# A hybrid decoder layer on one core: the mixers' small matmuls gathered in fewer places between the projections

## The chip, the cores and the metric

One core of a Trainium2 chip runs the whole layer as one program. The metric is device time in microseconds (us): the median of several executions of the program. The kernel before takes 152.27 us (three executions, 151.97 to 152.85).

## What is computed

One post-norm decoder layer on 256 tokens of width 1024, in float32. A first layer norm gives h; one input projection (1024 to 3844 columns) feeds four causal mixers of four heads each: a Mamba-2 SSD, HGRN2, RetNet retention and MoBA attention. Their outputs, each gated with SiLU, are put side by side and go through one output projection, and the result is normed with the residual.

```python
h = _layernorm(x, emb_ln_g, emb_ln_b)
proj = einsum('bld,dn->bln', h, w_in)
(s_z, s_xbc, s_dt, h_q, h_f, h_i, h_g, r_q, r_k, r_v, r_g,
 m_q, m_k, m_v, m_g) = split(proj)
y_cat = concatenate([_ssd(...), _hgrn2(...), _retention(...), _moba(...)])
out = _layernorm(ALPHA * h + einsum('blm,md->bld', y_cat, w_out), ln_g, ln_b)
```

## The kernel before

TensorE (PE in the profile) does two kinds of work. The projections are exact float32 products put together from three float32r products each (high part of x with high part of w, low with high, high with low): per half unit of 128 output columns or tokens, 8 k tiles times 3 matmuls of 128 x 256, recorded at line 406 as `pj_<unit>`. The mixers' own matmuls are small and in plain float32: attention scores, products with the values, transposes. Most use a half-width or half-height tile of the array (128 x 64, 64 x 64 or 64 x 128 in the profile's column behind the names); the transposes (`mpt`, `xst`, `yt`) and the segment sums (`seg`, `ecum`) use the whole 128 x 128.

The order of the work is written by hand and kept as written. The program walks through slots 0 to 29, one per half unit of the input projection, and then through the output projection, with a slot ahead of every second piece of it. `begin(slot)` first sends the load of a weight half six half units ahead (`load_w`, line 205, on SyncE's queue SP, five buffers), then splits the weight half four ahead into its high part (`split_hi`, line 222, on ScalarE, ACT) and, after the mixers' steps, its low part (`split_lo`, line 231, on VectorE, DVE). Between the two it runs the steps that the table `steps` lists for this slot. Then `project(slot)` emits the 24 matmuls. Each engine takes its instructions in this order, and waits on semaphores for what it reads and for the release of buffers. PSUM has eight banks, handed out in turn to whatever asks next; a bank is reused once its last reader is done.

The names that matter below, with their lines: `hgrn_diag` (486, output `pc`), `moba_tr(j)` (848: four transposes of the probabilities `pe` into a PSUM bank, `mpt`) and `moba_tr_in(j)` (852: ACT copies that bank out), `ssd_xt` (748, `xst`), `ssd_seg` (714 and 717, `seg`, `ecum`, which read `ra` from GpSimd, POOL, line 693), `ssd_scores_in` (734 `sm` on DVE, 736 `scx` on ACT), `hgrn_av` (438, `hgo`), `moba_av` (869, `mbo`), `ssd_av` (762 `ssy`, 766 `sso`), `ret_q` (895, `rq`), `ret_scores_in` (922, `rat`), `y_transpose` (417, `yt`) and `ret_av` (438, `reo`). The retention's decay table is loaded by `ret_load` (line 892) on the SP queue; its tile shares its memory with `pe`:

```python
    pe = sb([P, 3 * NH, P], "pe", tag="xt0")
...
    ret = sb([P, 2, 2, SEQ], "ret", tag="xt0")
...
    def ret_q():
        nc.vector.tensor_mul(rq, ps_of["r_q"], ret[:, 0])
```

Of the kernel before, what the change touches and what calls it, by code (L numbers as in the profile page):

```python
# [29 lines left out]
# Order of the branches in the output projection.  # L30
ORDER = [0, 1, 3, 2]

# Columns of w_in by unit, in the order of their use.
# [27 lines left out]
# Rows that are the same for every token.  # L61
# [10 lines left out]
# Column pieces of the output projection by token tile: the last ones are the smaller.  # L72
OCOLS = [(0, 512, 1024), (0, 512, 768, 1024)]

# Per-channel parameters: emb_g, emb_b (k tiles), conv_w (4 taps, 4 tiles), conv_b, lb logits.
# [3 lines left out]
# Shape constants.  # L79
# [40 lines left out]
def hybrid_layer(  # L120
# [49 lines left out]
    # The tensor engine runs at half its clock until it has been busy for some microseconds:  # L170
    # products of a cleared tile keep it so while x comes in.
# [11 lines left out]
    # The weights stream in halves of a unit; each half is split exactly into two float32r  # L183
    # parts. Those of the output projection also take the place of spent mixer tiles.
# [147 lines left out]
    ps_of, hq = {}, {}  # L332

    def first_unit():
        """Both halves of unit 0 side by side, as the k tiles come in."""
        ps = [bank(f"pj_h_f{n}")[:, :SEQ] for n in range(2)]
        ps_of["h_f", 0], ps_of["h_f", 1] = ps

        def part(k, q):
            l = (whi, whi, wlo)[q][0, k // 4][:, k % 4]  # L340
            r = (hhi, hlo, hhi)[q]
            for n in range(2):
                nc.tensor.matmul(ps[n], l[:, n * P:(n + 1) * P], r[:, k, :], start=(k == 0 and q == 0),  # L343
                                 stop=(k == KT - 1 and q == 2))
        for k in range(KT):
            if k < 4:
                h_transpose(k + 4, 0)
                h_transpose(k + 4, 1)
                h_in(k + 4)
            if k == 1:  # L350
                split_hi(0, 1, 2, (1,), nc.vector.tensor_copy)
            part(k, 0)
            if k:
                part(k - 1, 1)
        part(KT - 1, 1)
        split_lo(0, 0, 2, (1,))
        split_lo(0, 1, 2)
        split_hi(1, 0)
        split_hi(1, 1)
        project(2, (0, 1))  # L360
        for k in range(KT):
            part(k, 2)
        project(3, (0, 1))

    def project(slot, parts=(0, 1, 2)):
        """Half a unit: 128 columns (channels on partitions) or 128 tokens."""
# [45 lines left out]
    def y_transpose(y, idx):  # L412
        """y [tokens, T, 256] -> the two k tiles of y_cat, channels on partitions."""
        b = bank(f"yt{idx}").rearrange("p (a t) -> p a t", a=2)
        for j in range(2):
            for T in range(NT):
                nc.tensor.transpose(b[:, j, T * P:(T + 1) * P], y[:, T, j * P:(j + 1) * P], ident)
        ytb[idx] = b
# [6 lines left out]
    def hs(t, h, lo_, n_):  # L425
        """head h of [128 channels on two tiles, tokens]"""
        r = 64 * (h % 2)
        return t[r:r + 64, h // 2, lo_:lo_ + n_]
# [21 lines left out]
    # Softmax over the single layer, cumulated, less its first row.  # L450
# [23 lines left out]
    # The attention within 64 tokens is built level by level: at level m the keys of an  # L474
    # even block of m tokens meet the queries of the odd block that follows. Heads by
    # parity: index (h % 2, T, h // 2); each parity has its own PSUM bank.
# [149 lines left out]
    def conv(n, name):  # L626
        """causal convolution of channel tile n, straight from the projection"""
        ps = ps_of[name][:, n % 2, :]
        if n % 2 == 0:
            acc[name] = sb([P, 2, SEQ], f"cacc_{name}", tag="cacc", bufs=2)  # L630
        a_ = acc[name][:, n % 2, :]

        def tap(i):
            return ch[:, C_CW + 4 * i + n:C_CW + 4 * i + n + 1]
        nc.scalar.activation(a_, ps, AF.Identity, scale=tap(3), bias=ch[:, C_CB + n:C_CB + n + 1])  # L635
        for d in range(1, 4):
            nc.vector.scalar_tensor_tensor(a_[:, d:], ps[:, :SEQ - d], tap(3 - d), a_[:, d:],  # L637
                                           op0=ALU.mult, op1=ALU.add)
# [20 lines left out]
    def ssd_step_a():  # L659
        # softplus(u) = max(u, 0) + log1p(e), e = exp(-|u|); log1p(e) = 2 atanh(e / (2 + e))  # L660
        au = sb([P, 8], "au")
        sd["ex"] = sb([P, 8], "ex")
        sd["ea"] = sb([P, 4], "ea")
        nc.vector.scalar_tensor_tensor(au, u, -1.0, u, op0=ALU.mult, op1=ALU.max)
        nc.scalar.activation(sd["ea"], row("alog"), AF.Exp)
        nc.scalar.activation(sd["ex"], au, AF.Exp, scale=-1.0)

    def ssd_step_b():
# [22 lines left out]
        # operands of the segment sums: sum over r of [r > s] [r <= l] a_r  # L691
# [169 lines left out]
    def moba_av():  # L861
        """channels on partitions: what the output projection takes"""
# [104 lines left out]
    po = {}  # L967

    def oproj(i, T, c0, c1):
        """branch i's share of 128 tokens by columns c0 .. c1 (within 512)"""  # L970
# [18 lines left out]
    def out_norm(T):  # L989
# [9 lines left out]
        for cs in cuts:  # L999
# [5 lines left out]
    # Steps taken in each slot before its half unit of projection: what a step reads was  # L1005
    # put in order at least a slot before, so that the tensor engine does not wait for it.
# [4 lines left out]
        6: [lambda: hgrn_diag(qk, 0), moba_load],  # L1011
        7: [lambda: hgrn_diag(e1, 8), lambda: level(2), h_values, hgrn_diag_in],
# [12 lines left out]
        17: [lambda: load_rows(0), ssd_step_a, ssd_step_b, lambda: moba_tr(0)],  # L1025
        18: [level128, moba_v, ssd_scores, lambda: moba_tr(1), lambda: moba_tr_in(0), level128_in, ssd_scores_in],
        19: [ssd_xt, lambda: moba_tr(2), lambda: moba_tr_in(1)],
        20: [ssd_seg, ssd_exp, lambda: moba_tr_in(2), lambda: hgrn_av(0), lambda: hgrn_av(1),
             ret_load],
        21: [ret_q, ssd_xt_in, ssd_mask, hgrn_norm, moba_av, lambda: residual(0)],  # L1030
        22: [ssd_av, ret_k, lambda: residual(1), lambda: load_rows(2)],
        23: [ssd_gate, ssd_norm],
        24: [ret_v, ret_scores, ret_cross, ssd_out, ret_scores_in, ret_cross_in],
        25: [lambda: y_transpose(sy.rearrange("p (t h) d -> p t (h d)", t=2), 0),
             lambda: ret_av(0), lambda: ret_av(1)],
        26: [lambda: y_split(0), hgrn_out],
# [82 lines left out]
```

## Time and profile before

| | |
|---|---|
| executions | 152.27, 152.85, 151.97 us; median 152.27 |
| profiled execution, first to last instruction (span) | 150.6 us |
| PE busy | 138.5 us (92%), 1320 matmuls |
| DVE busy | 116.5 us (77%), 240 instructions |
| ACT busy | 74.8 us (50%), 120 instructions |
| POOL busy | 17.8 us (12%), 23 instructions |
| DMA | 26.07 MB, mean 173 GB/s |

The page of the profile gives the profiled execution by its span, 150.6 us, and no other time for it; the median of the runs lies 1.65 us above that span. Busy times of engines overlap each other, so they don't add up to the span. Rows of the timeline give start, duration, engine, line, operation, output and inputs, the tile of the array that a matmul uses, the shape, and how many equal instructions the row stands for; a wait before it stands in brackets. The end of a matmul in the trace is modelled, so durations of neighbours overlap, and the start of the next one is the better measure of what one costs.

### The profile page before, as it was taken

The numbers are of one execution on the slowest core, as the hardware profiler recorded it, in microseconds if no ns is written. First come the engines' busy times: TensorE is split into PE (matmuls) and PEld (weight loads), VectorE is DVE, ScalarE is ACT, GpSimd is POOL, SyncE is SP. The second block draws the span as 40 slices with busy tenths as digits, with TensorE's granted clock in tenths as the row PEclk, the third lists the DMA queues.
The fourth block names the chain that finished last, engine by engine and source line by source line (L and its number), as shares of the span: only waits on it lengthen the run. The fifth ranks groups of instructions, "written<-read, shape, count | busy, mean of one in ns | idle before, by whom it ended". The sixth has DMA issues, their size and how long they took to land.

```text
span 150.6 us, 3259 instructions
## 1 busy us (share of the span) xinstructions
PE 138.5 (92%) x1320; PEld 127.7 (85%) x1320; DVE 116.5 (77%) x240; ACT 74.8 (50%) x120; POOL 17.8 (12%) x23
## 2 busy tenths in 40 slices
PE   6859999999999999999999999998999999999900
PEld 3149999999999998999999999997999988888800
DVE  2589968988596397969899999859379899168681
ACT  3079978552451759699919722062663764000000
POOL 4230000000000000000062063050004000004040
PEclk9986999999999999999999999999999999999995
DMA  4998299998748431656517800689804450000304
GB/s 151 275 406 324 69 325 325 307 327 319 197 133 255 138 80 59 168 189 232 190 65 256 308 0 0 159 310 364 270 23 139 140 139 4 0 0 0 139 0 139
DMA packets 9390, 26.07 MB, mean 173 GB/s; under 512 B 1056, under 2 KB 1696, under 8 KB 9120
## 3 DMA queue, kind: packets, MB, share of 16 engines
q1 hardware_dynamic: 9376, 25.87, 52.2%
q8 instruction: 10, 0.16, 0.4%
q14 instruction: 4, 0.03, 0.1%
HBM read 24.82 MB, written 1.05 MB: 172 GB/s over the span
## 4 chain that ended last, share of the span: by engine, by line
PE 56%; DVE 20%; ACT 8%; DMA 6%; issue 3%; POOL 2%; SPq 1%; POOLq 1%; DVEq 0%; ACTq 0%
PE po L979 5%; PE po L980 5%; PE po L978 5%; PE pj_h_f L343 4%; PE pj_m_q L406 4%; PE pj_xs L406 4%; PE pj_m_k L406 4%; PE pj_m_g L406 4%; PE pj_h_q L406 4%; PE pj_h_i L406 4%; PE pj_r_g L406 4%; DMA xt<-in_x_dram 3%; DMA ret<-in_ret_dram 3%; PE pj_bc L406 2%; ACT pe L842 2%
## 5 line engine op out<-in xcount | busy, mean ns | idle before, releaser
L979 PE MATMUL po<-wlo_wo,yhi 128*128 128x512 f32 (+1 forms) x40 | 14.0, 349 | 0.0
L978 PE MATMUL po<-whi_wo,yhi 128*128 128x512 f32 (+1 forms) x40 | 14.0, 349 | 0.0
L980 PE MATMUL po<-whi_wo,ylo 128*128 128x512 f32 (+1 forms) x40 | 13.9, 347 | 0.0
L222 ACT CAST whi_wo<-wr_wo 128x1024 fp32r<-128x1024 f32 x8 | 8.3, 1047 | 5.3 <-PE pj_h_g L406 2.2
L231 DVE TENSOR_TENSOR wlo_wo<-wr_wo,whi_wo 128x1024 fp32r<-128x1024 f32 x8 | 9.6, 1218 | 0.0
L693 POOL TENSOR_SCALAR_AFFINE_SELECT ra<-ahi 128x1024 fp32r<-128x1024 f32 x1 | 1.1, 1101 | 65.6 <-DVE ahi L689 65.6
L978 PEld LDWEIGHTS po<-whi_wo,yhi 128*128 128x128 f32 x40 | 7.5, 188 | 1.0
L980 PEld LDWEIGHTS po<-whi_wo,ylo 128*128 128x128 f32 x40 | 7.5, 188 | 1.0
L979 PEld LDWEIGHTS po<-wlo_wo,yhi 128*128 128x128 f32 x40 | 7.5, 188 | 1.0
L986 DVE TENSOR_TENSOR xn<-xn,po 128x512 f32<-128x512 f32 (+1 forms) x5 | 2.9, 579 | 5.8 <-PE po L980 5.8
L176 PE MATMUL warm<-warm 128*128 128x512 f32 x6 | 5.5, 1082 | 1.5 <-DVE warm L173 1.5
L637 DVE SCALAR_TENSOR_TENSOR cacc_xs<-pj_xs,ch,cacc_xs 128x255 f32<-128x255 f32 (+2 forms) x6 | 2.9, 482 | 4.6 <-ACT cacc_xs L635 4.4
L300 PEld LDWEIGHTS tr<-ck,xn 128*128 128x128 f32 x16 | 2.3, 171 | 4.1 <-DVE xn L276 4.1
L300 PE MATMUL tr<-ck,xn 128*128 128x128 f32 x16 | 3.6, 351 | 2.3 <-DVE xn L276 2.3
L263 DVE BATCH_NORM_STATS2 lst<-xt 128x6 f32<-128x512 f32 x4 | 2.8, 694 | 3.6 <-DMA xt<-in_x_dram 3.6
L842 ACT ACTIVATE pe<-pe,mmax 128x128 f32<-128x128 f32 (+1 forms) x8 | 3.5, 445 | 3.0 <-DVE mmax L835 3.0
L176 PEld LDWEIGHTS warm<-warm 128*128 128x128 f32 x6 | 1.8, 326 | 3.6 <-issue 2.1
L222 ACT CAST whi_h_f<-wr_h_f 128x512 fp32r<-128x512 f32 x3 | 1.9, 617 | 6.1 <-DMA wr_h_f<-in_w_dram 6.1
L406 PE MATMUL pj_h_g<-whi_h_g,hhi 128*128 128x256 f32 x16 | 4.7, 294 | 0.0
L406 PE MATMUL pj_m_q<-hhi,whi_m_q 128*128 128x256 f32 x16 | 4.7, 293 | 0.0
L406 PE MATMUL pj_r_k<-hhi,whi_r_k 128*128 128x256 f32 x16 | 4.7, 293 | 0.0
L406 PE MATMUL pj_m_v<-whi_m_v,hhi 128*128 128x256 f32 x16 | 4.7, 292 | 0.0
(298 smaller groups left out, 544.7 us busy)
## 6 DMA issues: line engine op xcount, KB each, us to landing
wr_wo<-in_wo_dram SPq DMA_DIRECT2D x8, 512.0 KB, 4.0
rb<-in_rows_dram SPq DMA_DIRECT2D x2, 1024.0 KB, 7.7
wr_z<-in_w_dram SPq DMA_DIRECT2D x2, 520.0 KB, 6.3
xt<-in_x_dram SPq DMA_DIRECT2D x4, 256.0 KB, 3.4
wr_h_f<-in_w_dram SPq DMA_DIRECT2D x4, 256.0 KB, 5.2
wr_h_q<-in_w_dram SPq DMA_DIRECT2D x2, 512.0 KB, 5.2
wr_h_i<-in_w_dram SPq DMA_DIRECT2D x2, 512.0 KB, 5.0
wr_m_q<-in_w_dram SPq DMA_DIRECT2D x2, 512.0 KB, 4.9
```

The costliest lines, as they stand in the source:

```text
L176: nc.tensor.matmul(wb, warm[:, :P], warm, start=True, stop=True)
L222: copy(whi[i, j][:, r, :], t[:, r, :])
L231: nc.vector.tensor_sub(wlo[i, j][:, r, :], t[:, r, :], whi[i, j][:, r, :].bitcast(F32))
L300: nc.tensor.transpose(trb[k][:, T * P:(T + 1) * P], xn[T][:, k * P:(k + 1) * P], ident)
L343: nc.tensor.matmul(ps[n], l[:, n * P:(n + 1) * P], r[:, k, :], start=(k == 0 and q == 0), stop=(k == KT - 1 and q == 2))
L406: nc.tensor.matmul(ps, l, r, start=(n == 0), stop=(n == len(seq) - 1))
L637: nc.vector.scalar_tensor_tensor(a_[:, d:], ps[:, :SEQ - d], tap(3 - d), a_[:, d:], op0=ALU.mult, op1=ALU.add)
L842: nc.scalar.activation(pt[:, h, :], pt[:, h, :], AF.Exp, bias=mmax[:, i:i + 1], accum_out=msum[:, i:i + 1])
L978: nc.tensor.matmul(po[T, c0], yhi[:, k, ts], hi, start=(i == 0 and j == 0), stop=False)
L979: nc.tensor.matmul(po[T, c0], yhi[:, k, ts], lo, start=False, stop=False)
L980: nc.tensor.matmul(po[T, c0], ylo[:, k, ts], hi, start=False, stop=(i == 3 and j == 1))
L986: nc.vector.tensor_add(xn[T][:, cs], xn[T][:, cs], po[T, cs.start])
```

## The change

Only the table `steps` is edited (and comments are dropped). The first `hgrn_diag` goes from slot 6 to 7; `moba_tr(0)` and its copy from 17 and 18 to 18; `moba_tr_in(1)` from 19 to 18; `ssd_xt` and `moba_tr(2)` from 19 to 20; `moba_av` from 21 to 22; `y_transpose` of the SSD output and `ret_av` from 25 to 26. No instruction is added or removed. Small matmuls stood ahead of sixteen half units of the input projection, and now stand ahead of twelve; the one place within the output projection stays.

```diff
-        6: [lambda: hgrn_diag(qk, 0), moba_load],
-        7: [lambda: hgrn_diag(e1, 8), lambda: level(2), h_values, hgrn_diag_in],
+        6: [moba_load],
+        7: [lambda: hgrn_diag(qk, 0), lambda: hgrn_diag(e1, 8), lambda: level(2), h_values,
+            hgrn_diag_in],
...
-        17: [lambda: load_rows(0), ssd_step_a, ssd_step_b, lambda: moba_tr(0)],
-        18: [level128, moba_v, ssd_scores, lambda: moba_tr(1), lambda: moba_tr_in(0), level128_in, ssd_scores_in],
-        19: [ssd_xt, lambda: moba_tr(2), lambda: moba_tr_in(1)],
-        20: [ssd_seg, ssd_exp, lambda: moba_tr_in(2), lambda: hgrn_av(0), lambda: hgrn_av(1),
-             ret_load],
-        21: [ret_q, ssd_xt_in, ssd_mask, hgrn_norm, moba_av, lambda: residual(0)],
-        22: [ssd_av, ret_k, lambda: residual(1), lambda: load_rows(2)],
+        17: [lambda: load_rows(0), ssd_step_a, ssd_step_b],
+        18: [level128, ssd_scores, lambda: moba_tr(0), lambda: moba_tr(1), moba_v, level128_in,
+             ssd_scores_in, lambda: moba_tr_in(0), lambda: moba_tr_in(1)],
+        20: [ssd_xt, ssd_seg, ssd_exp, lambda: moba_tr(2), lambda: hgrn_av(0), lambda: hgrn_av(1),
+             lambda: moba_tr_in(2), ret_load],
+        21: [ret_q, ssd_xt_in, ssd_mask, hgrn_norm, lambda: residual(0)],
+        22: [moba_av, ssd_av, ret_k, lambda: residual(1), lambda: load_rows(2)],
         23: [ssd_gate, ssd_norm],
         24: [ret_v, ret_scores, ret_cross, ssd_out, ret_scores_in, ret_cross_in],
-        25: [lambda: y_transpose(sy.rearrange("p (t h) d -> p t (h d)", t=2), 0),
-             lambda: ret_av(0), lambda: ret_av(1)],
-        26: [lambda: y_split(0), hgrn_out],
+        26: [lambda: y_transpose(sy.rearrange("p (t h) d -> p t (h d)", t=2), 0),
+             lambda: ret_av(0), lambda: ret_av(1), lambda: y_split(0), hgrn_out],
```

How this moves instructions is shown at three places. The first is PE ahead of the first half of r_k (slot 20), of the kernel before:

```order
L406 MATMUL pj_r_q<-hhi,wlo_r_q_943 128x256
L714 MATMUL seg_1197<-ra_189,upr 128x512
L714 MATMUL seg_1197<-ra_190,upr 128x512
L714 MATMUL seg_1200<-ra_189,upr 128x512
L714 MATMUL seg_1200<-ra_190,upr 128x512
L717 MATMUL ecum<-a,ck 128x4
L438 MATMUL hgo<-hv,yh 64x64 x10
```

and of the changed kernel:

```order
L406 MATMUL pj_r_q<-hhi,wlo_r_q_943 128x256
L748 MATMUL xst<-ck,xc 128x128 x4
L714 MATMUL seg_1192<-ra_189,upr 128x512
L714 MATMUL seg_1192<-ra_190,upr 128x512
L714 MATMUL seg_1195<-ra_189,upr 128x512
L714 MATMUL seg_1195<-ra_190,upr 128x512
L717 MATMUL ecum<-a,ck 128x4
L848 MATMUL mpt_1203<-ck,pe 128x128 x4
L438 MATMUL hgo<-hv,yh 64x64 x10
```

`xst` and the third `mpt` stood one half unit earlier and are now in this place; the third `mpt`, the last reader of `pe`, is behind `ecum`. On the SP queue of the changed kernel the load of `ret`, which needs that memory, stands where it stood:

```order
L205 DMA wr_h_g_1153<-in_w_dram 128x1024 [waits DMAHW0_49,DVE_49,Activation_49]
L205 DMA wr_m_g_1183<-in_w_dram 128x1024 [waits DMAHW1_49,DVE_49,Activation_49]
L892 DMA ret<-in_ret_dram 128x1024 [waits PE_49]
L205 DMA wr_m_g_1262<-in_w_dram 128x1024 [waits DMAHW2_49,DVE_49]
L205 DMA wr_r_g_1306<-in_w_dram 128x1024 [waits DMAHW3_49,DVE_49]
```

Nothing moved on this queue, and the load's one wait is for PE.

The second place is PE around r_k's second half (slots 21 and 22); a piece of the difference:

```order
+L869 MATMUL mbo<-mpt,mv 64x128 x12
 L762 MATMUL ssy<-xdt,mm 64x64 x16
 L766 MATMUL sso<-xde,scx 128x128 x2
-L406 MATMUL pj_r_v<-whi_r_v_1096,hhi 128x256
-L406 MATMUL pj_r_v<-whi_r_v_1096,hlo 128x256
-L406 MATMUL pj_r_v<-wlo_r_v_1125,hhi 128x256
```

MoBA's product `mbo` stood 24 projection matmuls earlier, alone between two halves of r_k, and now stands right ahead of the SSD's.

The third place is PE around the second half of h_g (slots 25 and 26), of the kernel before:

```order
L406 MATMUL pj_h_g<-whi_h_g_1264,hlo 128x256
L406 MATMUL pj_h_g<-wlo_h_g_1293,hhi 128x256
L417 MATMUL yt_1477<-ck,sy 128x128 x4
L438 MATMUL reo<-rv,rat 64x64 x24
L406 MATMUL pj_h_g<-whi_h_g_1195,hhi 128x256
L406 MATMUL pj_h_g<-whi_h_g_1195,hlo 128x256
```

and of the changed kernel:

```order
L406 MATMUL pj_h_g<-whi_h_g_1264,hlo 128x256
L406 MATMUL pj_h_g<-wlo_h_g_1280,hhi 128x256
L417 MATMUL yt_1507<-ck,sy 128x128 x4
L438 MATMUL reo<-rv,rat 64x64 x24
L406 MATMUL pj_m_g<-hhi,whi_m_g_1308 128x256
L406 MATMUL pj_m_g<-hlo,whi_m_g_1308 128x256
```

The SSD output's transposes and the retention output now come behind both halves of h_g, 24 projection matmuls later. DVE, POOL and SP keep their order throughout. On ACT the copies of the first and second `mpt` now stand together behind `scx`: the first stood ahead of the copies of `level128_in`, the second behind a `whi` split.

## Rows read from the trace of the kernel before

**Rows 1.** The page, parts 1 and 2: busy time, and PE by fortieths of the span.
```profile
PE 138.5 (92%) x1320; PEld 127.7 (85%) x1320; DVE 116.5 (77%) x240; ACT 74.8 (50%) x120; POOL 17.8 (12%) x23
...
PE   6859999999999999999999999998999999999900
```
**Rows 2.** PE's waits: waiting line, releaser, us in total, times, longest.
```profile
PE reo L438 <- DVE rat L922: 0.4, 2, 0.2
```
**Rows 3.** The chain that ended last, 79 to 104 us: start, us, what.
```profile
79.34 4.41 DMA ret<-in_ret_dram
...
102.48 1.21 DVE rat L922 x2
```
**Rows 4.** Timeline of PE around the first `pc` (slot 6), and the second's last records.
```profile
29.77 0.28 PE L406 MATMUL pj_h_i<-wlo_h_i,hhi 128*128 128x256 f32 x1
29.98 0.63 PE L486 MATMUL pc<-ck,qk 128*64 128x2 f32 x16
...
30.77 0.29 PE L406 MATMUL pj_m_q<-hlo,whi_m_q 128*128 128x256 f32 x1
...
33.81 0.38 PE L486 MATMUL pc<-ck,e 128*64 128x2 f32 x8
```
**Rows 5.** Timeline of PE around `mbo` (slot 21).
```profile
85.92 0.28 PE L406 MATMUL pj_r_k<-hhi,wlo_r_k 128*128 128x256 f32 x1
86.13 1.53 PE L869 MATMUL mbo<-mpt,mv 128*64 128x128 f32 x24
...
87.05 0.61 PE L869 MATMUL mbo<-mpt,mv 128*64 128x128 f32 x8
...
87.81 0.28 PE L406 MATMUL pj_r_k<-hlo,whi_r_k 128*128 128x256 f32 x1
```
**Rows 6.** Timeline of PE around the first `mpt` (slot 17).
```profile
68.51 0.28 PE L406 MATMUL pj_m_v<-whi_m_v,hlo 128*128 128x256 f32 x1
68.63 0.28 PE L406 MATMUL pj_m_v<-wlo_m_v,hhi 128*128 128x256 f32 x1
68.75 0.60 PE L848 MATMUL mpt<-ck,pe 128*128 128x128 f32 x4
...
69.31 0.28 PE L406 MATMUL pj_m_v<-whi_m_v,hlo 128*128 128x256 f32 x1
```
**Rows 7.** Timeline of PE: `seg` and `hgo` (slot 20), `yt` and `reo` (slot 25).
```profile
80.42 1.09 PE L714 MATMUL seg<-ra,upr 128*128 128x512 f32 x4
...
81.56 0.80 PE L438 MATMUL hgo<-hv,yh 128*64 128x64 f32 x20
...
83.33 0.28 PE L406 MATMUL pj_r_k<-hlo,whi_r_k 128*128 128x256 f32 x1
...
102.30 0.28 PE L406 MATMUL pj_h_g<-wlo_h_g,hhi 128*128 128x256 f32 x1
...
103.73 1.50 PE L438 MATMUL reo<-rv,rat 128*64 128x64 f32 x44 [0.17 <-DVE rat L922]
...
105.39 0.28 PE L406 MATMUL pj_h_g<-whi_h_g,hlo 128*128 128x256 f32 x1
```
**Rows 8.** From issue to landing, weight halves of m_g and r_g (512 KB each).
```profile
DMA to landing us min/median/max: 3.5/3.9/4.3
...
DMA to landing us min/median/max: 4.6/6.7/8.7
```
**Rows 9.** Timelines of ACT and POOL: what slot 20's matmuls wait for.
```profile
79.26 0.60 ACT L736 COPY scx<-scg 128x128 f32<-128x128 f32 x2 [3.38 <-DVE sm L734]
...
77.77 2.07 POOL L693 TENSOR_SCALAR_AFFINE_SELECT ra<-alo 128x1024 fp32r<-128x1024 f32 x1
```
**Rows 10.** Timelines of ACT, DVE and PE: towards HGRN2's output and its transposes (slot 28).
```profile
106.77 1.05 ACT L222 CAST whi_wo<-wr_wo 128x1024 fp32r<-128x1024 f32 x1 [2.24 <-PE pj_h_g L406]
...
111.58 0.69 DVE L612 TENSOR_TENSOR ho<-ho,g_h_g 128x512 f32<-128x512 f32 x1
...
113.77 0.49 PE L417 MATMUL yt<-ck,ho 128*128 128x128 f32 x3
```

## The prediction

> **What bounds the kernel now.** I read the page first, then the list of PE's waits, then the chain that ended last, then the timeline of PE at each edited place. The page shows PE busy in 92% of the span; of the fortieths (3.77 us each) from 11 to 143 us all but one have nine tenths or more, and the one with eight is at 102 to 105 us [rows 1]. The list of waits shows one wait of PE between the projections: `reo` for the masked scores `rat` on DVE, 0.4 us in two pieces [rows 2]. So PE sets the end, and a matmul that starts earlier everywhere makes the end earlier, unless DVE falls behind. The chain tells how far DVE is from that: from 79 to 104 us it runs through the load of the decay table `ret`, then through DVE (with a turn over ACT and POOL) to `rat` [rows 3], and from there to `reo`. DVE has no slack in front of `reo`; PE reaches it just before DVE does. That load is the start of DVE's stretch: any delay of its landing arrives at `rat`.
>
> **What the change removes on PE.** No matmul goes. Two things can: what it costs PE to change between projections and small matmuls, and the wait at `reo`.
>
> The price of a change, from the starts on PE. Projection matmuls follow each other every 0.12 us [rows 6]. Around the first `pc`, 1.00 us pass from the last projection matmul before it to the second after it; two projection steps are 0.24. Sixteen records of `pc` last 0.63 and the last eight of the same shape 0.38 [rows 4], so eight cost 0.25 and sixteen 0.50. What is left, 0.26 us, is the way in and out. Around `mbo` it is 1.89 less 0.24, less 24 records at 0.115 (1.53 against 0.61 for 24 and 8 [rows 5]) = 1.38: 0.27 us. In the changed kernel `pc` stands ahead of the second `pc`, and `mbo` ahead of `ssy`, each in the same 128*64 tile as its new neighbour, so both prices go: **-0.26 and -0.27 us**. Bounds: 0 each, if the neighbour pays instead (no row shows these two pairs side by side), and 0.27 each.
>
> Around the first `mpt` the row says otherwise: 0.68 us from the last projection matmul to the second after it [rows 6], less 0.24, leaves 0.44. Four records last 0.60, one record of 128 columns 0.27 (0.61 less three steps of 0.115 [rows 5]), so a transpose costs 0.11 and four cost 0.44: the place itself costs nothing. The transposes use the whole 128*128 array, as the projections do. So slots 17 and 19, which hold only transposes, give back **0**. The Trainium skill, "TensorEngine Tiling (Array Packing)", section Key Properties, says why one would expect this: changing the tiling mode, not just the tile, drains TensorE. It speaks against two of the four merged places: counted by places, four at 0.265 would give 1.06 us; by that rule, as by the rows, it is 0.53.
>
> The wait. From the last h_g matmul ahead of `yt` to the second behind `reo` pass 3.09 us [rows 7]. Undisturbed it would be 0.12, four transposes at 0.11, half of a change of tile (0.13), and what the 48 records of the equal `hgo` take to the second matmul behind them, 1.77 [rows 7]: 2.46. So 0.63 is lost, of which the list books 0.4; the rest is queueing inside the two pieces. With 24 more projection matmuls ahead of it, PE comes 24 x 0.117 = 2.8 us later, and this goes: **-0.63 us** (at least 0.4), if DVE comes no later than PE.
>
> **What DVE and the load do.** `ret` lies in the memory of `pe`, whose last reader is the third `mpt`. That used to be done before 79.34, when the load was issued [rows 3]. Now: slot 20's place began at 80.42 [rows 7]; it begins 0.26 earlier by `pc` and 0.88 earlier because `xst` and the third `mpt` (eight transposes) come in it instead of before it: 79.28. Then `xst` 0.44, `seg` and `ecum` 81.56 - 80.42 = 1.14 [rows 7], and 0.60 to the last transpose's end: 81.46. The load goes out at about 81.5, 2.2 us later. From issue to landing it took 4.4 us with a half of m_g just ahead on the queue [rows 3]; the m_g halves took 3.5 and 4.3 [rows 8]. Now m_g's half is about 2.5 us ahead, so I take a value near the fast end, 3.7, and keep 3.5 to 4.6 (the faster r_g half [rows 8]). It lands at 85.2 in place of 83.75: DVE's stretch shifts by 1.45 us, and `rat` ends at 103.69 + 1.45 = 105.14.
>
> PE comes to `yt` at 102.30 + 0.12 + 2.8 - 0.53 = 104.69 and to `reo` at 104.69 + 0.44 + 0.13 = 105.26. That is 0.1 us after `rat`: no wait, but no more than that to spare. In general, with L us from issue to landing, **the new wait is L - 3.8 us**.
>
> **Costed at nothing, with their cover.** `seg` comes 0.7 us earlier; its second operand `ra` on POOL ends at 79.84 [rows 9], and PE needs it at 79.28 + 0.44 + 0.23 = 79.95. `hgo`'s bank, before that of `scx`, is now that of the first `mpt`, whose copy stands behind `scx` on ACT, which ends at 79.86 [rows 9]; `hgo` comes at 81.3, so 1.4 us are there for one copy. The copies of both `mpt` push a `whi` split back by about a copy, and with it a `wlo` on DVE; DVE waits for `ret` there in any case. The longer wait of the SP queue at `ret` holds back the second half of m_g and r_g, used slots later. Next to be late is `ho`, which feeds the transposes of slot 28: it ends at 112.27 and PE comes at 113.77 [rows 10], then 1.2 us earlier. DVE's shift reaches it through the late row and weight loads on ACT, but ACT stands 2.24 us waiting for PE's h_g on that path [rows 10], and h_g now ends earlier, so up to about 2.2 us of shift are hidden.
>
> **Sum.** 0.26 + 0.27 + 0.63 = 1.16 us against the profiled execution: 150.6 to about 149.4. The median of the runs stands 1.65 us above that span; I carry that over: 152.27 - 1.16 = **151.1 us**. A measurement of this kernel can tell some 0.5%, 0.76 us, from no change: faster means under 151.51, slower over 153.03.
>
> **Rivals.**
> - The load lands later than I take it, L from 3.9 to 4.6: the wait at `reo` comes back at 0.1 to 0.8 us, **151.2 to 151.9**. For it: `ret` itself took 4.4. Against: it had company then. Chance 0.20.
> - The changes of tile are not given back, because `pc` behind `pc` or `mbo` ahead of `ssy` pays them; only the wait goes: 152.27 - 0.63 = **151.6**. For it: no row has such a pair. Against: inside `hgo` and `reo` operands change all along at the same tile, at an even pace. Chance 0.08.
> - Every place has its price, transposes too: 4 x 0.265 + 0.63 = 1.69, **150.6**. Against: the first `mpt`'s rows. Chance 0.07.
> - Slower: the load of `ret` falls behind other transfers. Place: `reo`, through `rq` and the whole DVE stretch. The price is L - 3.8; it eats the gain at L = 5.0 and makes the kernel slower by over 0.5% from L = 5.7. The slow half of r_g took 8.7 [rows 8]; that would be a wait of 4.9 and **156.0**. Against: only halves of m_g are near it on the queue. Chance 0.07.
>
> **Chances and range.** The forecast case has 0.58, with its own range 150.8 to 151.4. Faster by over 0.5%: it (nearly all of it), the price per place, and the lower half of the late load, 0.70; slower 0.06 (L over 5.7); the rest, 0.24, within. The range runs from 150.5 (price per place) to 151.9 (the load at 4.6, and the changes not given back); the slow loads stay out.
>
> **What would show it.** Right: the list of PE's waits has no `reo`, or under 0.2 us; the load of `ret` issued at about 81.5 and landing by 85.3; `mbo` followed by `ssy` at 0.11 us, without a step; `seg` and `hgo` without waits; the first m_g matmul about 1.2 us earlier than before. Wrong: a wait at `reo` or `yt` for DVE, a wait of `hgo` for ACT, a wait of slot 28's transposes for `ho`, or an unchanged distance from `pc` or `mbo` to the matmuls around them.

## The result and the profile after

The changed kernel takes **150.55 us** (median of four executions, 150.22 to 150.74), the kernel before 152.27 (151.97 to 152.85). The ratio is **0.9891**, 95% interval 0.9864 to 0.9919: faster by 1.1%, 1.72 us, where 1.16 was forecast. The profiled execution took 150.22 us, with a span of 148.5. Two of the twelve executions of `pc` alone, 152.80 and 153.62 us, were over 1.5% slower than its fastest and are left out of its median and ratio below.

The page, parts 1 and 2 (busy time; PE by fortieths of the span):

```profile
PE 136.9 (92%) x1320; PEld 127.0 (86%) x1320; DVE 116.4 (78%) x240; ACT 74.7 (50%) x120; POOL 17.8 (12%) x23
...
PE   5679999999999999999999999999999999999800
```

The eight among the nines of [rows 1], at 102 to 105 us, is gone. PE's list of waits (waiting line, releaser, us in total, times, longest) is whole here; the line of `reo` of [rows 2] is not in it, and both lines left belong to the start:

```profile
PE tr L300 <- DVE xn L276: 2.2, 1, 2.2
PE warm L176 <- DVE warm L173: 1.5, 1, 1.5
```

The chain that ended last (start, us, what) was on the load of `ret` and on DVE in this stretch [rows 3]. It is on PE now, piece by piece:

```profile
78.62 0.44 PE xst L748 x4
79.05 0.94 PE seg L714 x4
79.99 0.12 PE ecum L717 x2
80.11 0.49 PE mpt L848 x4
80.60 1.55 PE hgo L438 x48
...
104.00 0.44 PE yt L417 x4
104.44 1.55 PE reo L438 x48
```

`seg` and `hgo`, whose cover was named in the prediction, follow without a wait. DVE's stretch and its start, from DVE's timeline and the view of the tile `ret`:

```profile
84.39 0.69 DVE L895 TENSOR_TENSOR rq<-pj_r_q,ret 128x512 f32<-128x512 f32 x1 [1.27 <-DMA ret<-in_ret_dram]
...
102.95 1.28 DVE L922 TENSOR_TENSOR rat<-rs,ck 128x512 f32<-128x512 f32 x2
```
```profile
L892 SPq DMA_DIRECT2D ret<-in_ret_dram x1: 328/328/328, 80.6 to 80.6; - x1
...
DMA to landing us min/median/max: 3.7/3.7/3.7
```

DVE waits 1.27 us for the table, and its next instruction behind `rat` starts at 104.14, just before PE's `reo` at 104.4: in time, with little to spare.

**A ruler that leaves the start out.** Spans of two executions can't be laid side by side without care: the first matmul of the h_i projection, which stands ahead of every edited place, starts at 24.24 us in the profile of before and at 23.48 in that of after. So I measure from it to the start of the last matmul, and call this the stretch. PE's timeline of the kernel before and of the changed one:

```profile
24.24 0.28 PE L406 MATMUL pj_h_i<-whi_h_i,hhi 128*128 128x256 f32 x1
...
142.46 0.28 PE L980 MATMUL po<-whi_wo,ylo 128*128 128x256 f32 x1
```
```profile
23.48 0.28 PE L406 MATMUL pj_h_i<-whi_h_i,hhi 128*128 128x256 f32 x1
...
140.34 0.28 PE L980 MATMUL po<-whi_wo,ylo 128*128 128x256 f32 x1
```

The stretch is 118.22 us before and 116.86 after: **-1.36**. The other 0.76 of the two spans' difference lies in the start; the last experiment comes back to it.

### The profile page after: what moved, and what is told of

Read it like the earlier page. It is cut to its first block, busy times and chain, and to the rows that moved or that the text cites. A ratio compares the mean times of both kernels' runs of the same rounds, so it can differ in the third digit from the quotient of the medians.

```text
span 148.5 us, 3256 instructions
## 1 busy us (share of the span) xinstructions
PE 136.9 (92%) x1320; PEld 127.0 (86%) x1320; DVE 116.4 (78%) x240; ACT 74.7 (50%) x120; POOL 17.8 (12%) x23
## 4 chain that ended last, share of the span: by engine, by line
PE 89%; DMA 3%; DVE 3%; SPq 1%; POOLq 1%; POOL 1%; issue 0%; DVEq 0%
PE po L979 5%; PE po L980 5%; PE po L978 5%; PE pj_h_f L343 4%; PE pj_z L406 4%; PE pj_xs L406 4%; PE pj_m_v L406 4%; PE pj_m_k L406 4%; PE pj_h_g L406 4%; PE pj_m_g L406 4%; PE pj_m_q L406 4%; PE pj_bc L406 4%; PE pj_r_k L406 4%; PE pj_r_g L406 4%; PE pj_h_i L406 4%; PE pj_r_v L406 4%
## 5 line engine op out<-in xcount | busy, mean ns | idle before, releaser
L176 PE MATMUL warm<-warm 128*128 128x512 f32 x6 | 4.6, 939 | 1.5 <-DVE warm L173 1.5
L776 ACT ACTIVATE ssq<-sy 128x512 f32<-128x512 f32 x1 | 0.6, 632 | 9.2 <-DVE sy L774 9.2
L406 PE MATMUL pj_z<-whi_z,hhi 128*128 128x260 f32 x16 | 4.6, 289 | 0.0
L406 PE MATMUL pj_m_k<-hhi,whi_m_k 128*128 128x256 f32 x16 | 4.6, 287 | 0.0
```

Source lines behind the costliest of these rows:

```text
L176: nc.tensor.matmul(wb, warm[:, :P], warm, start=True, stop=True)
L406: nc.tensor.matmul(ps, l, r, start=(n == 0), stop=(n == len(seq) - 1))
```

## The experiments

All twelve stand in one table, with the first measurement of each of the two kernels. The ratio is that to the kernel before, run beside them on the same chip; L is the time from issue to landing of the load of `ret`; the wait is PE's at `reo` by the list. Places in the text are given from the first h_i matmul of the same profile.

| kernel | median us | ratio, interval | h_i starts | stretch | L | wait |
|---|---|---|---|---|---|---|
| before | 152.27 | 1 | 24.24 | 118.22 | 4.4 | 0.4 |
| before, again | 151.94 | 1.0013, 0.9988 to 1.0038 | 23.23 | 118.33 | 4.6 | 0.5 |
| the change | 150.55 | 0.9891, 0.9864 to 0.9919 | 23.48 | 116.86 | 3.7 | none |
| the change, again | 150.09 | 0.9898, 0.9874 to 0.9923 | 23.15 | 116.82 | 3.6 | none |
| `pc` alone | 151.76 | 0.9979, 0.9955 to 1.0003 | 23.91 | 118.15 | 4.7 | 0.5 |
| `mbo` alone | 152.06 | 0.9998, 0.9979 to 1.0018 | 24.26 | 118.31 | 4.6 | 0.5 |
| transposes alone | 153.65 | 1.0110, 1.0074 to 1.0146 | 24.00 | 119.63 | 3.6 | 0.5, and 0.8 at `yt` |
| `reo` alone | 150.63 | 0.9918, 0.9892 to 0.9943 | 23.66 | 117.49 | 4.4 | none |
| all but the transposes | 150.49 | 0.9879, 0.9850 to 0.9909 | 23.77 | 116.83 | 4.5 | none |
| change, `ret` later | 151.55 | 0.9968, 0.9947 to 0.9989 | 23.53 | 117.65 | 4.7 | 0.5 |
| change, `ret` early | 150.18 | 0.9872, 0.9845 to 0.9898 | 23.27 | 116.82 | 5.9 | none |
| change, `hgo` moved | 150.05 | 0.9866, 0.9839 to 0.9892 | 23.54 | 116.51 | 3.6 | none |
| both of these | 150.09 | 0.9891, 0.9867 to 0.9915 | 24.05 | 116.51 | 6.0 | none |
| change, two places more | 151.08 | 0.9955, 0.9937 to 0.9972 | 23.48 | 117.59 | 3.5 | none |

### `pc` alone

```diff
-        6: [lambda: hgrn_diag(qk, 0), moba_load],
-        7: [lambda: hgrn_diag(e1, 8), lambda: level(2), h_values, hgrn_diag_in],
+        6: [moba_load],
+        7: [lambda: hgrn_diag(qk, 0), lambda: hgrn_diag(e1, 8), lambda: level(2), h_values, hgrn_diag_in],
```

> The kernel before, with the first pc alone moved from slot 6 to 7. Theory (the price of a change of tile is saved, and all that PE saves ahead of the load of ret moves DVE's stretch along with it): from the first h_i matmul to the first of m_q's second half pass 10.51 us before; here 0.26 to 0.32 less, and the time falls by as much, to about 152.0. The wait at reo stays as it was (0.4 in the list). Rival (the neighbour pays the change): 10.51 us as before, time 152.27.

PE's timeline has the first matmul of m_q's second half, in the kernel before and here:

```profile
34.75 0.39 PE L406 MATMUL pj_m_q<-hhi,whi_m_q 128*128 128x256 f32 x1
```
```profile
34.10 0.39 PE L406 MATMUL pj_m_q<-hhi,whi_m_q 128*128 128x256 f32 x1
```

The price is given back: 34.10 - 23.91 = 10.19 in place of 34.75 - 24.24 = 10.51 us, -0.32. But the stretch is only 0.07 shorter. In this profile the 0.32 goes again at `reo` (from the last h_g matmul ahead of `yt` to the second behind `reo` 3.39 us pass in place of 3.09), because the load of `ret`, though issued 0.32 earlier along with PE, took longer. Its chain, against the 4.41 us of [rows 3]:

```profile
78.68 4.72 DMA ret<-in_ret_dram
```

From the first h_i matmul, the table lands at 59.49 us here and at 59.51 in the kernel before. So the first half of the theory holds, and the rival falls. The second half ("the time falls by as much", and an unchanged wait) doesn't hold in this profile, where the late landing of the table takes the gain back. The times leave it open: the ratio stands for -0.32 us, and its interval, -0.68 to +0.05, holds both the whole gain and none.

### `mbo` alone

```diff
-        21: [ret_q, ssd_xt_in, ssd_mask, hgrn_norm, moba_av, lambda: residual(0)],
-        22: [ssd_av, ret_k, lambda: residual(1), lambda: load_rows(2)],
+        21: [ret_q, ssd_xt_in, ssd_mask, hgrn_norm, lambda: residual(0)],
+        22: [moba_av, ssd_av, ret_k, lambda: residual(1), lambda: load_rows(2)],
```

> The kernel before, with mbo alone moved from slot 21 to 22. Theory (the price is saved on PE, but rat on DVE sets when reo can begin, and it hangs on the load of ret, which is issued ahead of this place): PE comes to yt 0.27 to 0.36 us earlier and waits that much longer at reo, about 0.7 in place of 0.4 in the list; the time stays at 152.27 within 0.15. Rival (what PE saves is saved in the end): 151.9 to 152.0, the wait at reo as before. Second rival (the neighbour pays): nothing moves, neither yt nor the wait.

PE's timeline:

```profile
88.97 1.53 PE L869 MATMUL mbo<-mpt,mv 128*64 128x128 f32 x24
90.33 1.10 PE L762 MATMUL ssy<-xdt,mm 128*64 128x64 f32 x32
91.36 0.71 PE L766 MATMUL sso<-xde,scx 128*128 128x128 f32 x4
91.83 0.37 PE L406 MATMUL pj_r_v<-whi_r_v,hhi 128*128 128x256 f32 x1
```

r_v begins at 91.83 - 24.26 = 67.57 in place of 67.90, -0.33, and the first m_g matmul at 83.99 in place of 83.86: nothing is left of it behind `reo`, as the theory had it. The list books 0.5 us of wait, not the 0.7 expected, but the place takes 0.48 us more (3.57 in place of 3.09, from the last h_g matmul ahead of `yt` to the second behind `reo`). The 0.13 us more at m_g are put down to the load, which took 4.58 us, 0.17 longer than in [rows 3]. Both rivals fall: the neighbour does not pay, and the saving is not kept.

### The transposes alone

```diff
-        17: [lambda: load_rows(0), ssd_step_a, ssd_step_b, lambda: moba_tr(0)],
-        18: [level128, moba_v, ssd_scores, lambda: moba_tr(1), lambda: moba_tr_in(0), level128_in, ssd_scores_in],
-        19: [ssd_xt, lambda: moba_tr(2), lambda: moba_tr_in(1)],
-        20: [ssd_seg, ssd_exp, lambda: moba_tr_in(2), lambda: hgrn_av(0), lambda: hgrn_av(1),
-             ret_load],
+        17: [lambda: load_rows(0), ssd_step_a, ssd_step_b],
+        18: [level128, ssd_scores, lambda: moba_tr(0), lambda: moba_tr(1), moba_v, level128_in,
+             ssd_scores_in, lambda: moba_tr_in(0), lambda: moba_tr_in(1)],
+        20: [ssd_xt, ssd_seg, ssd_exp, lambda: moba_tr(2), lambda: hgrn_av(0), lambda: hgrn_av(1),
+             lambda: moba_tr_in(2), ret_load],
```

> The kernel before, with the transposes mpt and xst and their copies alone moved (slots 17 and 19 emptied, as in the change), reo left in slot 25. Theory (a place that holds only full-array transposes costs nothing; the third mpt now comes behind ecum, so ret is issued about 2.3 us later, lands 3.7 us after that, and rat and with it reo come about 1.65 us later): the wait at reo grows from 0.63 us lost to about 2.3, and the time rises by 1.65, to about 153.9. Rival (every place has its price): the same less 0.53, about 153.4. Second rival (the load of ret is hidden, DVE catches up): 152.27, or 151.7 if the places have a price too.

This part of the change, by itself, makes the kernel slower by 1.1%. Two views show both halves of the theory. The first r_k matmul stands behind all the places that the edit touches. PE's timeline has it in the kernel before, and here:

```profile
83.11 0.39 PE L406 MATMUL pj_r_k<-hhi,whi_r_k 128*128 128x256 f32 x1
```
```profile
82.84 0.39 PE L406 MATMUL pj_r_k<-hhi,whi_r_k 128*128 128x256 f32 x1
```

That is 58.84 us from the first h_i matmul, against 58.87 before: two places fewer, nothing gained. And the chain: the load is issued behind the third `mpt`, 57.40 us after the first h_i matmul in place of 55.10, and is quicker than before.

```profile
80.87 0.51 PE mpt L848 x4
81.38 0.02 issue
81.40 3.58 DMA ret<-in_ret_dram
```

It lands 1.47 us later (60.98 against 59.51), and PE now waits ahead of `yt` too:

```profile
103.06 1.02 PE L417 MATMUL yt<-ck,sy 128*128 128x128 f32 x4 [0.77 <-DVE sy L789]
104.45 0.34 PE L438 MATMUL reo<-rv,rat 128*64 128x64 f32 x4 [0.36 <-DVE rat L922]
```

The stretch is 1.41 us longer, where 1.65 was expected; with L at 3.7 as expected it would have been a tenth more.

### `reo` alone

```diff
-        25: [lambda: y_transpose(sy.rearrange("p (t h) d -> p t (h d)", t=2), 0),
-             lambda: ret_av(0), lambda: ret_av(1)],
-        26: [lambda: y_split(0), hgrn_out],
+        26: [lambda: y_transpose(sy.rearrange("p (t h) d -> p t (h d)", t=2), 0),
+             lambda: ret_av(0), lambda: ret_av(1), lambda: y_split(0), hgrn_out],
```

> The kernel before, with the SSD output's transposes and reo alone moved from slot 25 to 26. Theory (the wait for rat goes, as PE comes there 2.8 us later and DVE no later): no reo in the list of waits, time lower by 0.63 (as forecast) to 0.79 (as the trace of the change would have it), 151.5 to 151.65. Rival (what is lost there is reo's own pace, not the wait): the distance from yt to the second matmul behind reo stays at 3.09 less 0.12, time 152.2. Second rival (ho for slot 28's transposes becomes late): a wait of PE at slot 28, time between the two.

The wait is gone and the stretch 0.73 us shorter, within the theory's 0.63 to 0.79; PE's timeline has `yt`, `reo` and m_g in one run:

```profile
104.65 0.60 PE L417 MATMUL yt<-ck,sy 128*128 128x128 f32 x4
105.18 1.62 PE L438 MATMUL reo<-rv,rat 128*64 128x64 f32 x48
106.73 0.39 PE L406 MATMUL pj_m_g<-hhi,whi_m_g 128*128 128x256 f32 x1
```

The median fell by more, 1.36 us (interval of the ratio: 0.9 to 1.6 us), and 150.63 is below the 151.5 to 151.65 expected. What may move a median more than the stretch is taken up below.

### All but the transposes

The moves of `pc`, `mbo` and `reo` together, made to the kernel before; `mpt` and `xst` stay in slots 17 and 19.

> The kernel before with the moves of pc, mbo and reo, without that of the transposes (they stay in slots 17 and 19). Theory (the places that hold only transposes cost nothing, and PE meets no wait at reo, where rat now comes some 1.9 us earlier than it): from the first h_i matmul to the last matmul 116.86 us within 0.15, as in the changed kernel, and the time as there, 0.989 of the kernel before. Rival (every place has its price): 0.53 us more, 117.4.

PE's timeline, first and last matmul of the stretch:

```profile
23.77 0.28 PE L406 MATMUL pj_h_i<-whi_h_i,hhi 128*128 128x256 f32 x1
...
140.60 0.28 PE L980 MATMUL po<-whi_wo,ylo 128*128 128x256 f32 x1
```

116.83 us: the same stretch as the changed kernel's, 116.86 and 116.82. Against `reo` alone it is 0.66 shorter, 0.32 for `pc` and 0.33 for `mbo`: with the wait gone, both are kept to the end. The move of the transposes, the largest piece of the edit, is worth nothing, and spends the margin at `reo`.

### The load of `ret`, later and earlier

```diff
-             lambda: moba_tr_in(2), ret_load],
-        21: [ret_q, ssd_xt_in, ssd_mask, hgrn_norm, lambda: residual(0)],
+             lambda: moba_tr_in(2)],
+        21: [ret_load, ret_q, ssd_xt_in, ssd_mask, hgrn_norm, lambda: residual(0)],
```

> The changed kernel, with the load of ret issued behind the second half of m_g on the SP queue instead of ahead of it. Theory (the new wait at reo is the delay of the landing less the slack; the slack was forecast at 0.1 and is 0.2 to 0.3 by the trace of the change): from the first h_i matmul to ret's landing pass 60.8 us in the changed kernel; if it is 1 to 2 us more here, the wait at reo (with yt) is 0.75 to 1.75 and the stretch from the first h_i matmul to the last matmul, 116.86 us in the changed kernel, grows by as much. Rival (ret is off the path in the changed kernel, DVE catches up before rat): no wait at reo, 116.9 again.

The load was issued no later (80.64, it waits for the third `mpt` in any case), but with the second half of m_g sent just ahead of it (79.9), and it took 4.70 us in place of 3.67. DVE's and PE's timelines:

```profile
85.43 0.69 DVE L895 TENSOR_TENSOR rq<-pj_r_q,ret 128x512 f32<-128x512 f32 x1 [2.31 <-DMA ret<-in_ret_dram]
```
```profile
104.81 0.34 PE L438 MATMUL reo<-rv,rat 128*64 128x64 f32 x4 [0.36 <-DVE rat L922]
105.31 1.50 PE L438 MATMUL reo<-rv,rat 128*64 128x64 f32 x44 [0.17 <-DVE rat L922]
```

It lands at 61.81 us from the first h_i matmul, 0.99 later than in the changed kernel (60.82). The first m_g matmul comes 0.78 later (83.22 against 82.44). So the margin at `reo` was **0.2 us**, and what is beyond it arrives at the end: the stretch is 0.79 longer. The rival (DVE catches up) falls.

The other way round, in memory of its own and loaded in slot 16:

```diff
-    ret = sb([P, 2, 2, SEQ], "ret", tag="xt0")
+    ret = sb([P, 2, 2, SEQ], "ret")
...
-        16: [level64, lambda: widen(64), lambda: conv_silu("xs", 0), lambda: z_in(0), lambda: z_in(1),
+        16: [ret_load, level64, lambda: widen(64), lambda: conv_silu("xs", 0), lambda: z_in(0), lambda: z_in(1),
...
-             lambda: moba_tr_in(2), ret_load],
+             lambda: moba_tr_in(2)],
```

> The changed kernel, with ret in memory of its own (not that of pe) and its load issued in slot 16, long before it is needed. Theory (PE sets the end, the load was just in time): rq's wait for ret (1.27 us) goes, rat ends up to 1.2 us earlier, and the stretch from the first h_i matmul to the last matmul stays at 116.86 within 0.15, the time at 0.989 of the kernel before. Rival (the load still costs something on the path): 0.3 us or more less, 116.5 or below.

`rq` follows without a wait and `rat` starts at 101.32 - 23.27 = 78.05 us, 1.42 earlier than in the changed kernel (79.47), a little more than the wait that went. DVE's timeline:

```profile
82.77 0.68 DVE L895 TENSOR_TENSOR rq<-pj_r_q,ret 128x512 f32<-128x512 f32 x1
```

The stretch is 116.82, as before the edit. In the changed kernel the load costs nothing; a margin is all that this buys.

### `hgo` to `mbo` and `ssy`

```diff
-        20: [ssd_xt, ssd_seg, ssd_exp, lambda: moba_tr(2), lambda: hgrn_av(0), lambda: hgrn_av(1),
-             lambda: moba_tr_in(2), ret_load],
-        21: [ret_q, ssd_xt_in, ssd_mask, hgrn_norm, lambda: residual(0)],
-        22: [moba_av, ssd_av, ret_k, lambda: residual(1), lambda: load_rows(2)],
+        20: [ssd_xt, ssd_seg, ssd_exp, lambda: moba_tr(2), lambda: moba_tr_in(2), ret_load],
+        21: [ret_q, ssd_xt_in, ssd_mask, lambda: residual(0)],
+        22: [lambda: hgrn_av(0), lambda: hgrn_av(1), moba_av, ssd_av, ret_k, lambda: residual(1), lambda: load_rows(2)],
...
-        24: [ret_v, ret_scores, ret_cross, ssd_out, ret_scores_in, ret_cross_in],
+        24: [ret_v, ret_scores, ret_cross, ssd_out, ret_scores_in, ret_cross_in, hgrn_norm],
```

> The changed kernel, with hgo moved from slot 20 to 22, ahead of mbo (the same 128*64 tile), and its norm on DVE to the end of slot 24. Theory (one more change of tile in and out is saved wherever two places of this tile are put together, 0.32 and 0.34 us in the two runs that moved pc and mbo alone): from the first h_i matmul to the last matmul 116.5 to 116.6 in place of 116.86, time 0.987 of the kernel before. Rival (ho for slot 28's transposes or rat comes too late): a wait at yt of slot 28 or at reo, 116.86 or more. Second rival (the price in slot 20 belongs to seg and ecum, 128*128, not to hgo): 116.86, and no such wait.

A third place joined, and the same amount: the stretch is 116.51, -0.31 to -0.35 against the two profiles of the changed kernel. PE's timeline shows the three in a row:

```profile
86.20 0.80 PE L438 MATMUL hgo<-hv,yh 128*64 128x64 f32 x20
...
87.65 1.48 PE L869 MATMUL mbo<-mpt,mv 128*64 128x128 f32 x24
88.97 1.10 PE L762 MATMUL ssy<-xdt,mm 128*64 128x64 f32 x32
```

Neither rival shows: PE has no wait, and the saving is there. What is left in slot 20 is all full-array (`xst`, `seg`, `ecum`, `mpt`), and has no price to speak of: 1.98 us from the last r_q matmul to the second r_k one, two projection steps taken off, where the four groups take 0.44 + 0.94 + 0.12 + 0.49 = 1.99 by the changed kernel's chain above. With the early load of `ret` added:

> The changed kernel with both further edits: hgo in slot 22, and ret in memory of its own, loaded in slot 16. Theory (PE alone sets the end; the early load takes the spread of that load out of reach of reo, but gives no time): from the first h_i matmul to the last matmul 116.5 us, as with hgo moved alone, and the time 0.9865 of the kernel before within 0.002; rat ends over 2 us ahead of reo. Rival (the two add up, as their ratios of 0.9872 and 0.9866 beside 0.9891 would let one think): 0.985 or below, 116.3 or less.

The stretch is 116.51, as the theory has it, and the two edits do not add up; `rat` ends 1.8 us ahead of `reo`, a little less than expected. In time the gain is not resolved: 0.9866 for `hgo` alone, but 0.9891 with both (0.9865 within 0.002 was expected), and beside that run the changed kernel has the same median of 150.09. So these versions have the shorter stretch, and none is shown to be faster.

### The opposite: two places more

```diff
-        24: [ret_v, ret_scores, ret_cross, ssd_out, ret_scores_in, ret_cross_in],
+        24: [ret_v, ret_scores, ssd_out, ret_scores_in],
+        25: [ret_cross, ret_cross_in],
...
-             lambda: ret_av(0), lambda: ret_av(1), lambda: y_split(0), hgrn_out],
-        27: [ret_norm],
+             lambda: ret_av(0), lambda: y_split(0), hgrn_out],
+        27: [lambda: ret_av(1), ret_norm],
```

> The changed kernel with two more places, the opposite of the change: rx (64*128 tile) alone in slot 25, and the second half of reo (128*64 tile) alone in slot 27. Theory (every place with a tile smaller than the array costs a change in and out, about 0.32 us, whichever side is halved): both places cost 0.26 to 0.36 each, and the stretch from the first h_i matmul to the last matmul grows from 116.86 to about 117.5, time 0.5 to 0.7 us more than the changed kernel beside it. Rival (only a tile halved in its columns pays): the place of reo alone, 117.2. Second rival (the changes are hidden again, the price was something of pc and mbo): 116.9.

PE's timeline at the new places:

```profile
100.63 0.71 PE L917 MATMUL rx<-rq,rk 64*128 64x128 f32 x8
101.28 0.38 PE L406 MATMUL pj_h_g<-whi_h_g,hhi 128*128 128x256 f32 x1
```
```profile
108.33 1.15 PE L438 MATMUL reo<-rv,rat 128*64 128x64 f32 x32
109.41 0.38 PE L406 MATMUL pj_m_g<-hhi,whi_m_g 128*128 128x256 f32 x1
```

Without any wait in the list, the stretch grows by 0.77 against the changed kernel beside it. By `yt` (80.71 against 80.32 us from the first h_i matmul) 0.39 of it is there, the price of `rx` alone; the other 0.38 is that of the moved part of `reo` (32 of its 48 records). So tiles halved on either side pay, a little more than the 0.26 to 0.36 expected; both rivals fall. In time it is 0.99 us more, where 0.5 to 0.7 was expected.

### Both kernels once more

> The changed kernel as it is, once more, beside the two others. Theory (the start of the kernel, up to the first h_i matmul, varies from run to run and has nothing to do with the edits): from the first h_i matmul to the last matmul 116.86 us within 0.1, wherever that first matmul stands (23.48 us in the changed kernel's profile, 24.24 in that of the kernel before, 23.27 to 24.26 in the eight others); time 0.989 of the kernel before. Rival (the change itself brought it forward): it stands at 23.5 again, and the kernels with a later one are chance.

> The kernel before as it is, once more. Theory (its end hangs on the landing of ret: 4.41 us from issue in its profile, 4.40 to 4.72 in the four others that kept that place of the load): the stretch from the first h_i matmul to the last matmul is 118.2 us and as much more as the load takes over 4.41, so 118.2 to 118.5, and the first h_i matmul stands somewhere from 23.2 to 24.3 us. Rival (the load always takes the same, the excess of the measured gain over the 1.36 us of the traces lies in the start): 118.2 within 0.05, the first h_i matmul at 24.2 again.

The changed kernel repeats its stretch within 0.04 (116.82), at another start (23.15). The kernel before repeats its own up to `reo` (h_g begins at 75.26 us both times); there its load takes 4.6 us in place of 4.41, and the stretch is 118.33. And its first h_i matmul stands at 23.23, a whole us earlier than the same kernel's 24.24. DVE's timeline shows where most of that (0.85 us) comes from, the landing of x; first the profile of before, then the second one of the same kernel:

```profile
7.26 0.69 DVE L263 BATCH_NORM_STATS2 lst<-xt 128x6 f32<-128x512 f32 x1 [1.16 <-DMA xt<-in_x_dram]
```
```profile
6.41 0.69 DVE L263 BATCH_NORM_STATS2 lst<-xt 128x6 f32<-128x512 f32 x1 [0.37 <-DMA xt<-in_x_dram]
```

So the start of one and the same kernel varies by more than the 0.76 us, which need not be the change's, and both theories of these two runs hold, their rivals not. A small part of the change in the start isn't ruled out: the seven profiles that contain the whole change begin h_i at 23.50 us in the mean, the seven others at 23.87, each group spread over 0.9 to 1.0 us.

## Why the prediction was right

It said 151.1 us, 150.5 to 151.9, and a chance of 0.70 for faster by over 0.5%; measured were 150.55 and 1.1%. The mechanism is borne out, but the number was in part luck: 150.55 lies below the range of the forecast case itself (150.8 to 151.4) and only 0.05 us inside the whole range, whose lower end comes from the price of every place, a rival that the runs refute. Of the 0.56 us that the forecast of 1.16 missed, 0.20 are terms that were put too small, and 0.36 the stretch doesn't show. Step by step:

- **What bounds the kernel.** PE does, with DVE just behind `reo`. Right; `mbo` alone says it most sharply, since a third of a us gained on PE vanishes there, and so it does in the profile of `pc` alone.
- **`pc`, -0.26.** Mechanism right, size low: 0.32. The working gave sixteen records 0.50 us, twice the last eight of [rows 4]; in the joined place they add 0.47, which explains half of the difference; the rest isn't located. From the last projection matmul to `lv` it takes 1.24 us, and took 0.77 with the second `pc` alone (PE's timeline of the changed kernel):

```profile
31.80 0.28 PE L406 MATMUL pj_m_q<-hhi,wlo_m_q 128*128 128x256 f32 x1
32.01 0.64 PE L486 MATMUL pc<-ck,qk 128*64 128x2 f32 x16
32.50 0.61 PE L486 MATMUL pc<-ck,e 128*64 128x2 f32 x16
33.04 0.69 PE L531 MATMUL lv<-A,kk 64*64 64x64 f32 x32
```

- **`mbo`, -0.27.** The same: 0.33. Its records were put at 1.38 us (the prediction's 24 records at 0.115 are twelve pairs at 0.115; the product is right); the place with `ssy` grew by 1.31 (from the last r_k matmul to the second r_v 3.27 in place of 1.96), and `ssy` begins 0.11 us behind the last record of `mbo`, without a step, as the prediction's sign had it. `ssy` itself is through to `sso` in 1.03 us in place of 1.08, most of the difference: it probably no longer pays the way in.
- **Slots 17 and 19, 0.** Right: 0.03 us by the transposes alone, and no difference between 116.83 and 116.82. This refutes the rival of a price for every place, although that rival's 150.6 us is nearest to the measured time: its sum comes out close for other reasons (the next paragraph). Reading the tile column ahead of counting places was what mattered; the rule of the Trainium skill, "TensorEngine Tiling (Array Packing)", Key Properties, that changing the tiling mode drains TensorE, agrees with these runs on which places pay (0.31 to 0.39 us for one of smaller tiles, 0.00 to 0.03 for one of transposes).
- **The wait at `reo`, -0.63.** Right in kind; 0.73 by `reo` alone. Undisturbed, the place takes 2.42 us (from the last h_g matmul at 103.72 to the second m_g one at 106.14), not the estimated 2.46, so 0.67 of it was lost at the place itself.
- **The load and DVE.** L was taken as 3.7 and measured as 3.67; the margin was taken as 0.1 and measured as 0.2. The issue was forecast at about 81.5 and came at 80.63, which is 0.76 of start and 0.1 of error. The choice rested on the distance to the m_g half ahead on the queue, and the runs bear that out (below). The late rival's mechanism, a later table arriving at `reo` one for one, is real: the run with `ret` later shows 0.79 us at the end of 0.99 at the landing, and the transposes alone show that it can make the kernel slower.
- **Covers.** `ra`, the copies behind `scx` and `ho` held: `ho` ends at 110.06 us, 1.6 us ahead of slot 28's transposes at 111.65.

The terms as measured, 0.32 + 0.33 + 0 + 0.73 = 1.38, are the stretch's 1.36. The medians differ by 1.72 and, in the second comparison, by 1.63 (151.72 to 150.09). What remains beyond the stretch, 0.36 us in the first and 0.12 in the second (where the stretches of the repeated profiles differ by 1.51), is not settled; the stretch's 1.36 and 1.51 lie within the intervals that the ratios give (1.2 to 2.1 and 1.2 to 1.9 us), so it may be nothing. The start varies by up to 1.1 us from profile to profile and may leave a part of itself in medians of a few runs. And the runs of the kernel before hang on a load that took 4.4 to 4.7 us in its six profiles with that place, where the changed kernel has a margin: the profiled execution of before had 4.41, nearly the shortest of the six, so others may have waited longer. That was not shown execution by execution, and the ranges of the runs side by side (151.24 to 152.31 for before, 149.85 to 150.84 for the change) are too alike to tell.

What the sum could have said, and did not: its terms hold only together. By the stretch the four parts alone make -0.07, +0.09, +1.41 and -0.73, in sum +0.70, and together -1.36. (The -0.07 and +0.09 are of single profiles, each with its own L.) Moving `reo` is what lets the saving of `mbo` through, and that of `pc` whatever the load does, and what pays for the late table.

## What to carry to other kernels

Count changes of the tile shape, not places: here a place of 64-wide or 64-high tiles between full-array matmuls cost 0.31 to 0.39 us of PE, a place of full-array transposes nothing, so only the former are worth joining. Two smaller tiles of different shape in one place save less: in the kernel before, `pc` (128*64) alone takes 0.76 us beyond two projection steps and `lv` (64*64) alone 0.81 (40.33 to 41.38), but both in one place 1.38 (33.35 to 34.97), so that 0.19 is saved. Where another engine arrives at a join just after PE, first move that join back; until then a saving on PE ahead of it can be lost there, as that of `mbo` was. And when a step moves that releases a buffer, follow the load that waits for the buffer through to its consumer: of this change the transposes' move gained nothing and cost 1.3 us of landing, covered with 0.2 us to spare.

## What the runs showed of the hardware

The same 512 KB load on the same queue took 3.5 to 3.7 us from issue to landing where the half of m_g ahead of it was sent 2.7 us earlier (the change, its repeat, the transposes alone and two others), and 4.4 to 4.7 where a half of m_g was sent 0.4 to 0.7 us earlier (the six profiles with the old order of `pe`'s transposes, and `ret` later). Moving this load by some two us therefore delayed its landing by less: by 1.31 us from the kernel before to the change, and by 1.00 between their repeats. The distance to the load ahead is not all of it: issued in slot 16, 0.4 us behind a half of r_v, the same load took 5.9 and 6.0 us, and no run shows why.

Small matmuls of one tile shape are cheaper in company: the 24 records of `mbo` added 1.31 us next to `ssy`, where 1.65 went with them alone, and 1.38 would be the pace of their records.

The start of one and the same program, up to its first h_i matmul, differed by 1.0 us between two executions (24.24 and 23.23), more than half of this change's effect, while the distance between two PE instructions far apart repeated to 0.04 us where no wait lay between them.
